# The order of projection products on TensorE during a linear recurrence

## The chip, the cores and the metric

The kernel runs on one core of one Trainium2 chip. The metric is the device time of one execution in microseconds (us). Engines: TensorE (PE; its weight loads are PEld), VectorE (DVE), ScalarE (ACT), GpSimd (POOL, which here mostly issues transfers) and SyncE (SP, which issues transfers).

## The reference

Two residual layers over 528 tokens (16 prepended and 512 of the input) of width 2048, in float32. The first layer is a convolution module beside a sparse attention; the change does not touch it. The second is a gated linear recurrence (HGRN2) of 16 heads of width 128. The part of it that matters here:

```python
def odd_mixer(hn, w_in, lb, norm_g, w_out):
    q, fz, i, g = split_last(hn @ w_in, (D_REC, D_REC, D_REC, D_REC))
    log_f = jnp.logaddexp(jnp.log(lb), jnp.log1p(-lb) + jax.nn.log_sigmoid(fz))
    k = (1.0 - lb) * jax.nn.sigmoid(-fz)
    o = hgrn2_chunkwise(heads(jax.nn.silu(q)), heads(log_f), heads(k), heads(i))
    o = o * lax.rsqrt(jnp.mean(jnp.square(o), -1, keepdims=True) + RMS_EPS)
    ...
    return o @ w_out

# hgrn2_chunkwise, one step over a chunk of tokens:
    b = jnp.cumsum(g_c, axis=2)
    o_inter = jnp.einsum('bhtk,bhkv->bhtv', q_c * jnp.exp(b), state)
    attn = jnp.einsum('bhtk,bhtsk,bhsk->bhts', q_c, jnp.exp(diff), k_c)
    o_intra = jnp.einsum('bhts,bhsv->bhtv', attn, v_c)
    state = (jnp.exp(b_last)[..., None] * state
             + jnp.einsum('bhsk,bhsv->bhkv', k_c * jnp.exp(b_last[:, :, None] - b), v_c))
```

`fz` (the forget gate) and `i` (called `v` in the kernel) are the two projections that are made head by head while the recurrence runs. `q` and `g` are made before it.

## The kernel before

Each float32 operand of a large product is split into a high and a low half in float16, and a product is three matmuls for each of its contraction steps: high by high (L214), high by low (L215) and low by high (L216). Weights come by transfers into a raw float32 tile. ACT rounds it to the high half `wh` and DVE takes the difference as `wl` (L174 and L175 for plain stripes, L1369 and L1370 for pairs). There are three buffers of `wh` and `wl`, and three PSUM banks `mps` that take the products' results in turn.

The recurrence is the loop over heads, `fz` and `v` of each head first and then the head itself (`rec_head`).

- The odd heads use `projections`: two plain stripes, for `fz` (j = 0) and for `v` (j = 2). A stripe is two column parts of 264 tokens by two halves of the contraction, four products of 24 matmuls. DVE takes `fz` out of its banks, ACT takes `v` out (L1013).
- The even heads from 2 on use `paired`: both projections by one Strassen step, seven products of 24 matmuls, 272 columns each, in the order 1, 5, 2, 4, 6, 7, 3. Their weights are sums and differences of the quarters of both stripes. POOL's accumulating transfers make the sums (L1382, L1386, L1389), and the weight tiles hold the products' weights in the pairs 1 and 5, 2 and 4, 7 and 6, and 3 alone. ACT takes products 1, 5 and 4 out of PSUM (L1401, L1403 for the two that go to `v`), DVE the others, with `u` as the running sum.
- `rec_head` does the recurrence of a head: float16 key-query matmuls of 64 columns (L1195 to L1197, results `s`, of which ACT and DVE make the attention tile `A`), float32 transposes of `v` (L1231, with the copy to `vt` by ACT, L1229), state matmuls (`st`, L1332, which need `kk` of ACT L1328) and outputs (`po`, L1343 and L1344, squared by ACT into `so`, L1350). ACT and DVE also make the gates (`ta`, `tb`), the decayed keys and queries (`kt0h`, `kt1h` and their low halves) between these.

Every engine runs its instructions strictly in its own order. That order is not the source's: a scheduler makes it from the dependences, its own picture of the times, and priorities, which the code gives in bands (`WGT` for weights, `EVAC` for taking results out of PSUM, `SIDE` for the head's own work). The seven products of `paired` are called inside the `EVAC` band, the products of plain stripes outside. So before the change the scheduler starts products of a pair while the odd head's `v` stripe in front of it still has matmuls left.

Of the kernel before, what the change touches and what calls it, by code (L numbers as in the profile page):

```python
# [74 lines left out]
def trunk_kernel(ctx: ExitStack, tc: tile.TileContext, x: bass.AP, w: bass.AP, wukv: bass.AP,  # L75
# [3 lines left out]
    V, S, G, P, Q = nc.vector, nc.scalar, nc.gpsimd, nc.tensor, nc.sync  # L79

    def band(level):
        return tc.high_priority(level * 1000000)
# [66 lines left out]
        V.tensor_scalar(vec[:, V_RG:V_RG + 16], vec[:, V_RG:V_RG + 16], 0.5, None, op0=OP.mult)  # L149


    loaded, halved = [], []

    def weight_tiles():
        return [wpool.tile([128, 2064], F16, name=n, bufs=3)[:, :2048] for n in ("wh", "wl")]
# [24 lines left out]
    def weights_of(at, items):  # L180

        if at % 2 == 0 or not ahead:
            ahead.clear()
            for i, half in enumerate(load_two([product_weights(*it) for it in items[at:at + 2]])):
                ahead[at + i] = half
        return ahead[at]
# [16 lines left out]
    def stripe_half(weights, X, parts, n, half, m=128):  # L203

        hi, lo = weights
        for o, sl in parts:
            products(o[:m], hi, lo, [[x[:, sl] for x in X[half * 8 + k]] for k in range(8)], n == 0, n == 1, m)

    def products(o, hi, lo, X, start, stop, m=128):

        issued = []
        for k, (xh, xl) in enumerate(X):
            ws = slice(k * 128, k * 128 + m)
            P.matmul(o, hi[:, ws], xh, start=start and k == 0, stop=False)  # L214
            P.matmul(o, hi[:, ws], xl, start=False, stop=False)  # L215
            issued.append(P.matmul(o, lo[:, ws], xh, start=False, stop=stop and k == len(X) - 1))  # L216
        return issued

    def evac(dst, parts, rstd):
# [208 lines left out]
    for k in range(KT):  # L428
        xh, xl = X0[k]
        st, sp = k == 0, k == KT - 1  # L430
        for parts, s, m in ((kwp, S_KW, KWM), (c0p, S_C, 128)):
            hi, lo = first[s][k // 8]
            ws = slice(k % 8 * m, k % 8 * m + m)
# [480 lines left out]
    for at, (pr, m) in enumerate(turns):  # L914
        u, c0, c1 = us[pr], C[pr], C[8 + pr]
        o = (mps if at % 7 < 3 else ps1)()[:, :HT]
        with band(WGT):
            hi, lo = weights_of(at, [(EPAIRS[p], m2) for p, m2 in turns])
        products(o, hi, lo, forms0[FORM[m]], True, True)
        with band(EVAC):  # L920
            if m == 2:
# [37 lines left out]
    def on_tile(k, wide=False):  # L959
        t = hp.tile([128, T if k < 6 or k in (12, 14) else SEQ], F32, name=f"on{k}", bufs=1)  # L960
        return t if wide else t[:, :SEQ]
# [83 lines left out]
    def strassen(turns, pairs, results, finished):  # L1045
# [5 lines left out]
        for n, (m, pr) in enumerate(turns):  # L1051
            o = (mps if made[0] % 7 < 3 else ps1)()[:, :HS]
            with band(WGT):
                hi, lo = weights_of(n, items)
            made[0] += 1
            products(o, hi, lo, [[x[:, NM:] for x in pair] for pair in gforms[FORM[m]]], True, True)
            if made[0] % 3 == 2:
                paced_steps(lsteps, 1, o, gpp)
# [58 lines left out]
    def head_inputs(h):  # L1117
        fz, v = [ht([128, T], F32, name, 2) for name in ("fz", "v")]
        if h in QT and h not in QDRAM:
            return fz, QT[h], v  # L1120
        q = ht([128, SEQ], F32, "q", 2)
        if h in QT:
            G.dma_start(q, qd[QDRAM.index(h)])
        return fz, q, v
# [289 lines left out]
    for h in range(16):  # L1414
        if h < 2:
            inputs[1] = inputs[1] or head_inputs(1)
        else:
            inputs[h] = head_inputs(h)
        fz, q, v = inputs[h]
        if h:  # L1420
            (paired if h in PAIRED else projections)(h, fz, v)
        if h in (8, 9):
            ON.append(on_tile(h))
            G.dma_start(ON[h], gd[h - 8])
        with band(SIDE):
            rec_head(h, fz, q, v)
# [166 lines left out]
    for at, (pr, m) in enumerate(turns):  # L1593
        n0, n1 = 2 * pr, 2 * pr + 1
        o = (mps if at % 7 < 3 else ps1)()[:, :HS]
        with band(WGT):
            hi, lo = weights_of(at, [(OPAIRS[p], m2) for p, m2 in turns])
# [6 lines left out]
        issued = products(o, hi, lo, forms[FORM[m]], True, True)  # L1604
# [126 lines left out]
```

## Time and profile before

| | |
|---|---|
| median of 3 runs | 1782.55 us (1781.63 to 1782.58) |
| profiled execution | 1785.19 us |
| its span | 1783.4 us |
| mean TensorE clock granted | 0.982 |
| recurrence with its projections, about | 1080 to 1600 us of the span |

The rows quoted below are of the profiled execution. A row of a timeline gives the start in us, the duration in us, engine, line, operation, the tile written and the tiles read, the shape, and in brackets the idle time just before it and what ended that. A row of waits gives the total in us, how often, and the longest. A row of windows gives the length of the stretch, the busy time of PE, PEld, DVE, ACT and POOL with their instructions, the granted clock (1.00 is full), the share of the transfer engines, and GB/s. Line numbers are those of the kernel before. In the changed kernel the same lines stand one further down (L215 to L217 for the three matmuls) or three (L1016 for L1013, L1372 for L1369, L1404 for L1401).

### The profile page before, as it was taken

How to read it: one execution, taken by the hardware profiler on the slowest of the kernel's cores; microseconds unless marked ns; L12 is line 12 of the kernel's file. 1: busy time of each engine (PE TensorE's matmuls, PEld its weight loads, DVE VectorE, ACT ScalarE, POOL GpSimd, SP SyncE). 2: the span in 40 equal slices, each digit the busy share in tenths (PEclk: the TensorE clock that was granted, in tenths of full speed). 3: DMA queues.
4: the chain of work that ended last, by engine and by line, in shares of the span. 5: the costliest groups of instructions: out<-in, count | busy, mean ns of one | idle time of the engine just before them, and what ended most of it. 6: DMA issues, size and time to landing. Idle time of an engine off the chain costs nothing. (4 is left out here: it accounts for less than half of the span.)

```text
span 1783.4 us, 37905 instructions
## 1 busy us (share of the span) xinstructions
PE 1730.9 (97%) x15616; PEld 1451.5 (81%) x15616; DVE 1442.3 (81%) x2412; ACT 967.1 (54%) x1782; POOL 293.8 (16%) x501
## 2 busy tenths in 40 slices
PE   9999999999999999999999999899999999989997
PEld 8775688888888888888888888787887787657886
DVE  7699899999478579699776587788888888879876
ACT  7333532235446455457534456666776777756553
POOL 1020233123342211102110101111111111100000
PEclk9999999999999999999999999999999999989998
DMA  9578688979999857877899978677677766524764
GB/s 361 171 235 268 176 237 201 251 227 232 233 247 303 209 185 273 252 253 264 277 281 297 290 237 236 181 188 195 153 193 181 188 159 181 158 80 151 261 217 141
DMA packets 108126, 393.34 MB, mean 221 GB/s; under 512 B 14768, under 2 KB 22616, under 8 KB 106096
## 3 DMA queue, kind: packets, MB, share of 16 engines
q0 software_dynamic: 36944, 157.91, 37.9%
q1 hardware_dynamic: 70720, 232.81, 36.9%
q8 instruction: 122, 2.00, 0.4%
q14 instruction: 52, 0.43, 0.1%
q10 hardware_dynamic: 288, 0.19, 0.0%
HBM read 369.07 MB, written 136.53 MB: 284 GB/s over the span
## 5 line engine op out<-in xcount | busy, mean ns | idle before, releaser
L215 PE MATMUL mps<-xl,wh 128*128 128x264 f16 (+3 forms) x2560 | 730.2, 285 | 1.6 <-DVE xl L242 1.6
L216 PE MATMUL mps<-xh,wl 128*128 128x264 f16 (+3 forms) x2560 | 730.2, 285 | 0.0
L214 PE MATMUL mps<-xh,wh 128*128 128x264 f16 (+3 forms) x2560 | 728.8, 286 | 0.0
L174 ACT ACTIVATE wh<-w 128x2048 f16<-128x2048 f32 (+1 forms) x174 | 331.0, 1902 | 306.7 <-PE mps L215 202.7
L175 DVE SCALAR_TENSOR_TENSOR wl<-w,wh 128x2048 f16<-128x2048 f32 (+1 forms) x174 | 396.9, 2281 | 113.8 <-ACT wh L174 113.4
L215 PEld LDWEIGHTS <-wh 128*128 128x128 f16 x4128 | 406.4, 98 | 100.6 <-issue 20.3
L216 PEld LDWEIGHTS <-wl 128*128 128x128 f16 x4128 | 406.5, 98 | 85.6 <-issue 3.1
L214 PEld LDWEIGHTS <-wh 128*128 128x128 f16 x4128 | 406.7, 99 | 81.7 <-issue 1.0
L632 DVE SCALAR_TENSOR_TENSOR z<-u,vec,z 128x528 f32<-128x528 f32 x240 | 179.3, 759 | 2.1
L214 PE MATMUL mps<-gh,wh 128*128 128x272 f16 (+1 forms) x368 | 108.1, 294 | 18.4 <-ACT v L1013 17.0
L289 POOL DMA_DIRECT2D ws<-in_w_dram x116 | 106.5, 1123 | 113.0 <-DMA ws<-ws 65.0
L215 PE MATMUL mps<-gl,wh 128*128 128x272 f16 (+1 forms) x368 | 108.0, 293 | 0.0
L216 PE MATMUL mps<-gh,wl 128*128 128x272 f16 (+1 forms) x368 | 107.8, 293 | 0.0
L1369 ACT ACTIVATE wh<-w 128x2048 f16<-128x2048 f32 (+1 forms) x28 | 47.6, 1699 | 62.9 <-DMA w<-in_w_dram 32.1
L216 PE MATMUL s<-xh,wl 128*128 128x256 f16 (+1 forms) x288 | 78.8, 274 | 0.0
L214 PE MATMUL s<-xh,wh 128*128 128x256 f16 (+1 forms) x288 | 78.8, 274 | 0.0
L215 PE MATMUL s<-xl,wh 128*128 128x256 f16 (+1 forms) x288 | 78.8, 274 | 0.0
L1370 DVE SCALAR_TENSOR_TENSOR wl<-w,wh 128x2048 f16<-128x2048 f32 (+1 forms) x28 | 56.5, 2018 | 20.8 <-ACT wh L1369 20.5
L331 POOL MEMSET pace<- 128x1 f32 x52 | 5.9, 113 | 352.9 <-ACT pace L330 352.9
L695 POOL DMA_DIRECT2D L<-mask x32 | 30.3, 947 | 165.0 <-DMA L<-bdram 104.3
L1318 DVE TENSOR_TENSOR kq<-kq,e 128x512 f32<-128x512 f32 (+1 forms) x80 | 55.5, 693 | 1.1
L222 DVE SCALAR_TENSOR_TENSOR gt<-mps,rstd 128x264 f32<-128x264 f32 (+1 forms) x70 | 31.2, 447 | 24.9 <-PE mps L216 24.6
(659 smaller groups left out, 3345.0 us busy)
## 6 DMA issues: line engine op xcount, KB each, us to landing
ws<-in_w_dram POOLq DMA_DIRECT2D x158, 512.0 KB, 8.4
w<-in_w_dram SPq DMA_DIRECT2D x72, 1024.0 KB, 7.5
w<-in_w_dram SPq DMA_DIRECT2D x118, 512.0 KB, 5.3
w<-ws SPq DMA_DIRECT2D x116, 512.0 KB, 4.9
ws<-ws POOLq DMA_DIRECT2D x58, 512.0 KB, 5.3
w<-in_w_dram POOLq DMA_DIRECT2D x28, 512.0 KB, 6.1
ws<-in_w_dram SPq DMA_DIRECT2D x16, 512.0 KB, 8.1
sq<-mbd POOLq DMA_DIRECT2D x16, 264.0 KB, 4.1
```

The costliest lines, as they stand in the source:

```text
L174: halved[:] = [S.activation(hi[:, :n], w32[:, :n], AF.Copy, scale=WS), V.scalar_tensor_tensor(lo[:, :n], w32[:, :n], WS, hi[:, :n], op0=OP ...
L175: V.scalar_tensor_tensor(lo[:, :n], w32[:, :n], WS, hi[:, :n], op0=OP.mult, op1=OP.subtract)]
L214: P.matmul(o, hi[:, ws], xh, start=start and k == 0, stop=False)
L215: P.matmul(o, hi[:, ws], xl, start=False, stop=False)
L216: issued.append(P.matmul(o, lo[:, ws], xh, start=False, stop=stop and k == len(X) - 1))
L222: V.scalar_tensor_tensor(dst[:, sl.start - o:sl.stop - o], p[:dst.shape[0]], IW, rstd[:dst.shape[0], sl], op0=OP.mult, op1=OP.mult)
L289: return G.dma_start(wsum[pair, m], src, accum_op=OP.add, max_dma_last_dim=4096)
L632: V.scalar_tensor_tensor(z, u[:, j:j + T], col(V_CW + i * CW + j), z, op0=OP.mult, op1=OP.add)
L695: return G.dma_start(biased[h, t][:, :wk(t)], M[t], accum_op=OP.add)
L1318: V.tensor_tensor(both, both, by, op=OP.mult)
L1369: halved[:] = [S.activation(hi[:, :n], raw[:, :n], AF.Copy, scale=WS), V.scalar_tensor_tensor(lo[:, :n], raw[:, :n], WS, hi[:, :n], op0=OP ...
L1370: V.scalar_tensor_tensor(lo[:, :n], raw[:, :n], WS, hi[:, :n], op0=OP.mult, op1=OP.subtract)]
```

## The change

A list `stream` is filled between heads 1 and 15. While it is, the first matmul of each product is told to stand on TensorE behind the last matmul of the product before it in the source. It concerns the scheduler's order alone.

```diff
-    loaded, halved = [], []
+    loaded, halved, stream = [], [], []
...
         for k, (xh, xl) in enumerate(X):
             ws = slice(k * 128, k * 128 + m)
-            P.matmul(o, hi[:, ws], xh, start=start and k == 0, stop=False)
+            with tc.issue_after(stream[-1].ins) if stream[1:] and k == 0 else ExitStack():
+                P.matmul(o, hi[:, ws], xh, start=start and k == 0, stop=False)
             P.matmul(o, hi[:, ws], xl, start=False, stop=False)
             issued.append(P.matmul(o, lo[:, ws], xh, start=False, stop=stop and k == len(X) - 1))
+        if stream:
+            stream.append(issued[-1])
         return issued
...
         if h:
+            if h == 1:
+                stream.append(None)
             (paired if h in PAIRED else projections)(h, fz, v)
+            if h == 15:
+                stream.clear()
```

TensorE has the same matmuls in both kernels, and SP's order is the same. TensorE's order differs from head 1 on; ACT's and DVE's differ with it, POOL's in a few rows.

In the rows that follow the numbers behind names tell tiles apart: `mps_19454` is the bank of the last part of head 13's `v` stripe; of head 14's pair, `mps_19824` is product 1, `mps_19850` product 5, `mps_19902` product 4, `mps_19928` product 6 and `mps_19982` product 3.

TensorE where head 14's pair begins. Before:

```order
L216 MATMUL mps_19454<-xh_9531,wl_19457 128x264
L214 LDWEIGHTS wh_19456
L214 MATMUL mps_19454<-xh_9566,wh_19456 128x264
L215 LDWEIGHTS wh_19456
L215 MATMUL mps_19454<-xl_9567,wh_19456 128x264
L214 LDWEIGHTS wh_19802
L214 MATMUL mps_19824<-xh_9456,wh_19802 128x272
```

and now:

```order
L216 MATMUL mps_19454<-xl_10265,wh_19456 128x264
L217 LDWEIGHTS wl_19457
L217 MATMUL mps_19454<-xh_10264,wl_19457 128x264
L215 LDWEIGHTS wh_19802
L215 MATMUL mps_19824<-xh_9456,wh_19802 128x272
L216 LDWEIGHTS wh_19802
L216 MATMUL mps_19824<-xl_9457,wh_19802 128x272
```

Product 1 started in the middle of the `v` stripe's last part (contraction tile `xh_9566` of the first half), and now starts behind its last matmul (`xh_10264`).

ACT around the copies out of PSUM of heads 13 and 14. Before:

```order
L1369 ACTIVATE wh_19819<-w32_19797 128x1024
L1350 ACTIVATE so_18424,ss_18425<-po_18402 128x128 x4
L1229 ACTIVATE vt0_13706<-sv_19126,rt1n_13703 128x128
L1251 ACTIVATE kt1h_13717<-kq1_13709 128x2x8x32
L1191 ACTIVATE kt0h_13713<-kq0_13705 128x256
L1251 ACTIVATE kt0h_13713<-kq0_13705 128x512
L1351 ACTIVATE ss_18425<-ss_18425,eps_r_78 128x4
L174 ACTIVATE wh_20250<-w32_20249 128x2048
L1013 ACTIVATE v_19344<-mps_19454 128x264
L1401 ACTIVATE v_19794<-mps_19850 128x264
L1403 ACTIVATE v_19794<-mps_19902 128x264
```

and now:

```order
L174 ACTIVATE wh_20356<-w32_20355 128x2048
L1353 ACTIVATE so_18424,ss_18425<-po_18402 128x128 x4
L1232 ACTIVATE vt0_13706<-sv_19126,rt1n_13703 128x128
L1313 ACTIVATE A_18697<-s1_18814 32x4x32
L1254 ACTIVATE kt0h_13713<-kq0_13705 128x512
L1194 ACTIVATE kt0h_13713<-kq0_13705 128x256
L1313 ACTIVATE A_18697<-s1_18814 32x4x32
L1313 ACTIVATE A_18697<-s1_18814 64x4x64
L1215 ACTIVATE ta_19559<-ta_19559 128x528
L1354 ACTIVATE ss_18425<-ss_18425,eps_r_78 128x4
L1404 ACTIVATE v_19794<-mps_19850 128x264
L1406 ACTIVATE v_19794<-mps_19902 128x264
```

The copy of the `v` stripe's last part (L1013) stood directly ahead of those of products 5 and 4 and has moved far ahead of these rows; the split of the second stripe of head 15 (`wh_20356`) stood behind the copies and now stands in front of them, where it takes the weight buffer that product 7 leaves.

TensorE just ahead of product 3 of head 14, now:

```order
L1198 MATMUL s1_18814<-kt1l_13718,kt1h_13717 128x64
L1199 LDWEIGHTS kt1h_13717
L1199 MATMUL s1_18814<-kt1h_13717 128x64
L1200 LDWEIGHTS kt1l_13718
L1200 MATMUL s1_18814<-kt1h_13717,kt1l_13718 128x64
L1234 MATMUL sv_19135<-ident_73,v_18894 128x128
L215 LDWEIGHTS wh_19819
L215 MATMUL mps_19982<-xh_10005,wh_19819 128x272
```

The transpose of head 13's `v` (`sv_19135`) stood in front of product 6 before, behind the `v` stripe's last matmul, and now stands in front of product 3.

ACT behind head 8's pair. Before:

```order
L174 ACTIVATE wh_17655<-w32_17654 128x2048
L1369 ACTIVATE wh_18002<-w32_17997 128x2048
L1251 ACTIVATE kt1h_13717<-kq0_13705 128x2x128x2
L1310 ACTIVATE A_16000<-s1_16117 32x4x32 x2
L1310 ACTIVATE A_16000<-s1_16117 64x4x64
L1203 ACTIVATE ta_17309<-fz_17091 128x528
L1204 ACTIVATE ta_17309<-ta_17309 128x528
L1205 ACTIVATE ta_17309<-ta_17309 128x528
L1328 ACTIVATE kk_16153<-st_16148 128x512
```

and now:

```order
L174 ACTIVATE wh_17655<-w32_17654 128x2048
L1194 ACTIVATE kt0h_13713<-kq0_13705 128x512
L1372 ACTIVATE wh_18002<-w32_17997 128x2048
L1254 ACTIVATE kt1h_13717<-kq0_13705 128x2x128x2
L1313 ACTIVATE A_16000<-s1_16117 32x4x32 x2
L1313 ACTIVATE A_16000<-s1_16117 64x4x64
L1331 ACTIVATE kk_16153<-st_16148 128x512
```

The split of head 10's first weights (`wh_18002`) stands ahead of `kk` in both. On TensorE the state matmuls that need `kk` stood behind 48 matmuls of head 9's `fz` stripe, and now stand behind 30.

## The prediction

> **What bounds the kernel now.** I read the totals first, then TensorE's waits in the recurrence (1080 to 1580 us), then the engines' rows around the longest wait.
>
> ```profile
> PE 1730.9 (97%) x15616; PEld 1451.5 (81%) x15616; DVE 1442.3 (81%) x2412; ACT 967.1 (54%) x1782; POOL 293.8 (16%) x501
> ```
>
> TensorE is the bound, and the change gives it no matmul more or less. So only its idle time and its clock can move. The waits are few:
>
> ```profile
> PE mps L214 <- ACT v L1013: 17.0, 5, 3.4
> PE sv L1231 <- ACT vt L1229: 4.9, 1, 4.9
> ...
> PE mps L214 <- ACT v L1403: 1.4, 1, 1.4
> ```
>
> The columns are total us, times and the longest. The five 3.4s stand in heads 6, 8, 10, 12 and 14, the 4.9 in head 2, the 1.4 in head 4. Each 3.4 also costs clock:
>
> ```profile
> 1176.68 0.28 PE L214 MATMUL mps<-gh,wh 128*128 128x272 f16 x1 [1.42 <-ACT v L1403]
> ...
> 1232.51 0.39 PE L214 MATMUL mps<-gh,wh 128*128 128x272 f16 x1 [3.40 <-ACT v L1013]
> 1232.69 0.43 PE L215 MATMUL mps<-gl,wh 128*128 128x272 f16 x1
> ...
> 1238.35 0.28 PE L216 MATMUL mps<-gh,wl 128*128 128x272 f16 x1
> ...
> 1238.70 0.28 PE L216 MATMUL mps<-gh,wl 128*128 128x272 f16 x1
> ```
>
> ```profile
> 1232.50:1238.30 5.80, 5.79 (x26) 3.90 (x26) 5.80 (x10) 4.18 (x12) 0.84 (x1) 0.50 1.05 299
> ...
> 1294.00:1355.50 61.50, 58.14 (x626) 50.39 (x626) 51.49 (x90) 42.99 (x99) 10.52 (x16) 0.94 0.68 175
> ```
>
> In the windows' rows the clock is the third number from the end: 0.50 for the 5.84 us from 1232.51 to 1238.35, so 2.9 us of work lost, and 0.94 over a whole pair of heads (61.50 us). After the idle of 1.42 matmuls run at full rate at once. Rows at full clock stand 0.116 us apart (1238.35 to 1238.70, three steps).
>
> Why 3.4: product 6 of a pair needs the third PSUM bank, which the last part of the odd head's v stripe leaves by ACT's copy L1013. ACT's queue holds it up:
>
> ```profile
> 1349.46 0.38 PE L1343 MATMUL po<-st,kq 128*128 128x128 f32 x2
> 1349.68 0.39 PE L1344 MATMUL po<-vt,A 128*128 128x128 f32 x2
> ...
> 1351.94 0.33 PE L1231 MATMUL sv<-ident,v 128*128 128x128 f32 x1
> ```
>
> ```profile
> 1349.54 1.06 ACT L1369 ACTIVATE wh<-w 128x1024 f16<-128x1024 f32 x1 [2.68 <-PE mps L215]
> 1350.50 0.26 ACT L1350 ACTIVATE so<-po 128x128 f32<-128x128 f32 x1
> ...
> 1351.50 0.38 ACT L1229 ACTIVATE vt<-sv,rt1n 128x128 f32<-128x128 f32 x1
> 1351.75 0.65 ACT L1251 ACTIVATE kt1h<-kq 128x512 f16<-128x512 f32 x1
> 1352.27 0.51 ACT L1191 ACTIVATE kt0h<-kq 128x256 f16<-128x256 f32 x1
> 1352.62 0.78 ACT L1251 ACTIVATE kt0h<-kq 128x512 f16<-128x512 f32 x1
> 1353.24 0.30 ACT L1351 ACTIVATE ss<-ss,eps_r 128x4 f32<-128x4 f32 x1
> 1353.41 1.92 ACT L174 ACTIVATE wh<-w 128x2048 f16<-128x2048 f32 x1
> 1355.21 0.40 ACT L1013 ACTIVATE v<-mps 128x264 f32<-128x264 f32 x1
> ...
> 1356.37 0.63 ACT L1212 ACTIVATE ta<-ta 128x528 f32<-128x528 f32 x1
> 1356.90 0.61 ACT L1251 ACTIVATE kt1h<-kq 128x512 f16<-128x512 f32 x1
> ```
>
> The weight split of W3 starts ACT at 1349.54, when product 4 gives up a weight buffer. The copy comes out 5.67 us later (1349.54 to 1355.21), and TensorE's last work before it starts at 1351.94 and takes 0.33: idle 3.40. The steps between these starts are my durations: so x4 1.00, vt 0.25, kt1h 0.52, kt0h 0.35 and 0.62, ss 0.17, wh 1.80, v 0.27, ta 0.53.
>
> **The change, part by part.** It adds no wait, no instruction and no transfer. It only tells the scheduler that from head 1 to 15 a product's first matmul stands behind the previous product's last one. What moves:
>
> 1. The v stripe no longer has paired products in its middle. Its banks empty before the pair, so the five waits on L1013 and the 1.42 on L1403 cannot come in this form: between a bank's products stand two others, 48 matmuls by 0.116 = 5.6 us. The copy it waits for then decides, and ACT's order has moved too.
>
> 2. Heads 10, 12 and 14. Behind product 7, ACT's next row is now the next stripe's split (wh L174, for which product 7 must have freed the weights), then so x4, then vt, and TensorE's next transpose (L1234 in the new lines) needs that vt: 1.80 + 1.00 + 0.25 = 3.05, with 0.15 for the hand-over (the 0.2 us between 1355.48, the end of v's 0.27, and the matmul at 1355.67 bounds it) 3.2. TensorE has only two po steps (0.22 each, 1349.46 to 1349.68) and eight key-query matmuls left, under 0.8 together. Idle 2.4. Then product 3 waits for product 5's bank, whose copy (L1404 now) stands behind A x3, kt0h twice, ta and ss: 0.83 + 0.62 + 0.35 + 0.53 + 0.17, and its own 0.27 and 0.2: 2.97, less the transpose's 0.27: idle 2.7. Together 5.1 where 3.40 was: +1.7 each, **+5.1**. The 0.83 for A is from this fence:
>
> ```profile
> 1369.14 1.91 ACT L1369 ACTIVATE wh<-w 128x2048 f16<-128x2048 f32 x1 [3.23 <-DMA w<-in_w_dram]
> 1370.96 0.67 ACT L1251 ACTIVATE kt1h<-kq 128x512 f16<-128x512 f32 x1
> 1371.53 0.92 ACT L1310 ACTIVATE A<-s 32x128 f32<-32x128 f32 x3
> 1372.36 0.63 ACT L1203 ACTIVATE ta<-fz 128x528 f32<-128x528 f32 x1
> ...
> 1374.24 0.58 ACT L1328 ACTIVATE kk<-st 128x512 f32<-128x512 f32 x1
> 1374.72 0.72 ACT L1210 ACTIVATE kq<-tb,logk 128x528 f32<-128x528 f32 x1
> ```
>
> 3. Head 6 has the same order, but some 0.8 us more of work in front of each of the two waits (more po pairs and key-query matmuls): idle 2.0 + 2.3 = 4.3, **+0.9**.
>
> 4. Heads 4 and 8. There the copies stand early in ACT's queue and nothing of point 2 arises. But behind the pair ACT reaches the split of the next pair's first weights (wh L1372) before kk, and TensorE now has only 30 product matmuls ahead of the state matmuls that need kk, where it had 48. The split waits for loads:
>
> ```profile
> 1109.17 0.87 POOL L1389 DMA_DIRECT2D w<-in_w_dram  x1 [2.51 <-DVE wl L1370]
> ...
> 1164.09 1.42 POOL L1389 DMA_DIRECT2D w<-in_w_dram  x1
> ```
>
> ```profile
> 1114.53 1.06 ACT L1369 ACTIVATE wh<-w 128x1024 f16<-128x1024 f32 x1 [3.64 <-DMA w<-in_w_dram]
> 1130.24 1.91 ACT L1369 ACTIVATE wh<-w 128x2048 f16<-128x2048 f32 x1 [7.85 <-DMA w<-in_w_dram]
> 1175.30 1.06 ACT L1369 ACTIVATE wh<-w 128x1024 f16<-128x1024 f32 x1 [8.58 <-DMA w<-in_w_dram]
> ```
>
> ```profile
> 1116.87 0.33 SPq L1380 DMA_DIRECT2D w<-in_w_dram  x1
> ...
> 1352.90 0.34 SPq L1380 DMA_DIRECT2D w<-in_w_dram  x1
> ```
>
> ```profile
> 1371.08 2.29 DVE L1370 SCALAR_TENSOR_TENSOR wl<-w,wh 128x2048 f16<-128x2048 f32 x1 [0.63 <-ACT wh L1369]
> w<-in_w_dram POOLq DMA_DIRECT2D x28, 512.0 KB, 6.1
> ```
>
> From T0, the end of the v stripe: the split of W7 and W6 takes 1.80 + 2.29; POOL's addition for W3 5.4 (1109.17 to 1114.53) to 11.2 (1164.09 to 1175.30), I take the page's median 6.1; W3's split 2.3: T0 + 12.5. The loads and the addition that follow take 13.4 (1116.87 to 1130.24) to 16.3 (1352.90 to 1369.14): T0 + 26 to 29. kk ends 1.80 + 0.57 + 0.83 + 0.48 = 3.7 later, T0 + 29.6 to 32.5. TensorE gets there after seven products (168 x 0.116 = 19.5), 1.7 of small matmuls and 5.3 of the 30 product matmuls and the small ones among them: T0 + 26.5. Idle 3.1 to 6.0; I take 4.4, near the middle, since the rows give no reason for either end. Head 8: 4.4 for 3.40, **+1.0**. Head 4: 4.4 for 1.42, and 2.9 of clock that was not lost before, **+5.9**.
>
> 5. Head 2's 4.92 comes from the wait of 7.85 on loads above, ahead of the first pair; the loads' order on SP is unchanged: 0, from -1 to +1.5. The end of the recurrence: 0, ±3. Elsewhere the new order leaves TensorE margins of 0 to 1 us behind its evacuations on DVE and ACT: 0, up to +1 for each of seven pairs.
>
> Clock: every pair of heads that had a 3.4 still has one stretch of idle time of that size or more, so its 2.9 stays. If both parts of point 2's idle time drop the clock apart, up to 2.9 more; if neither does, 2.9 less (the second rival).
>
> The sum is 5.1 + 0.9 + 1.0 + 5.9 = **+12.9**. The profiled execution took 1785.19 us (span 1783.4), so the changed kernel's would be 1798; the runs' median is 2.6 below it, 1782.55, and gives **1795**. A measurement of this kernel tells about 0.2% (3.6 us) from no change: faster is below 1779, slower above 1786.
>
> **The rivals.**
>
> *The stalls vanish (the other side).* If ACT reaches v's copies within the 5.6 us that two products take, the five waits go, 17.0, with their five losses of clock, 14.5: -31.5, 1751. For it: each bank's product ended 5.6 us earlier. Against it: the copy L1404 stands behind a split that itself waits for product 7, the very product in front of the one that needs the bank; it can come no sooner than 1.80 after it. It decides at product 3 of heads 10 to 14: if ACT's split is past before product 7 ends. Chance 0.08.
>
> *The idle time is there but in parts too short to drop the clock.* The idle of 1.42 dropped nothing, 3.40 did. If 2.0 to 2.7 do not, heads 10, 12 and 14 give 5.1 - 3.4 - 2.9 = -1.2 each, head 6 gives 0.9 - 2.9 = -2.0; with +1.0 and +5.9 that is +1.3: 1784, no change. For it: no row between 1.42 and 3.40 shows which way it goes. Against it: between the two parts TensorE does a single transpose of 0.27, so 5.4 us hold 0.3 of work. Chance 0.10. The Trainium skill, page "TensorE: Matmul & The Clock Gate", Part 1 (the HAM clock gate), has the clock fall after at least one wholly idle window of about 3.4 us, and the window runs freely. By that rule two gaps under 2.8 us would leave the clock up, and the sum would be this rival's. Here a gap of 3.40 dropped the clock five times in five, which a free-running window wholly without work could do only by luck, so the trace speaks for a rule that drops sooner.
>
> *W3's sum lands late everywhere.* Product 7's bank needs DVE's sum u, which now stands behind W3's low half; with 11.2 for POOL's addition in place of 6.1 it is up to 4.9 late, at four places 20: 1815. One of the two rows has it so. Against it: the row of 11.2 lay beside POOL's stripe loads, and the median of 28 is 6.1. Chance 0.13.
>
> **How the numbers follow.** The forecast's own case has 0.69, with 1785 to 1806 as its own range (heads 4 and 8 from 3.1 to 6.0, the margins of point 5). Below 1779 lie the first rival and a third of the second: 0.11. Within 0.2% lie the rest of the second and the lowest part of the forecast: 0.11. Slower: 0.78. The range from 1780 to 1812 leaves out the first rival, the low edge of the second and half of the third, 0.18 together.
>
> **What would show it.** Right: waits of TensorE at the transpose for vt (about 2.4) and at a product for v L1404 (about 2.7), in heads 10, 12 and 14 one behind the other; ACT's wh L174 released by TensorE just behind product 7; wh L1372 waiting for loads after heads 4 and 8, with TensorE waiting for kk; none for v L1016 any more; as much time at clock 0.50 as before, or more. Wrong: no wait at product 3 (the split came early), full clock behind the two parts, or product 7 waiting for u.

## The result, and the profile after

The changed kernel takes 1798.43 us (median of 4 runs, 1797.19 to 1800.05) beside 1782.57 for the kernel before on the same chip: a ratio of 1.0084, 95% interval 1.0065 to 1.0104, so 0.65 to 1.0% slower. Its profiled execution took 1798.05 us with a span of 1796.3, 12.9 more than the one of before.

The totals of the changed kernel's page:

```profile
PE 1733.2 (96%) x15616; PEld 1454.0 (81%) x15616; DVE 1442.6 (80%) x2412; ACT 970.7 (54%) x1782; POOL 292.6 (16%) x501
```

TensorE does the same 15616 matmuls, busy 2.3 us longer in the whole span; the rest of the 12.9 is idle time. Its windows over most of the recurrence show the same, before (from 1080 to 1565) and after (1080 to 1578):

```profile
1080.00:1565.00 485.00, 461.59 (x4854) 390.26 (x4853) 398.51 (x682) 338.01 (x739) 76.42 (x120) 0.96 0.70 183
```

```profile
1080.00:1578.00 498.00, 459.90 (x4817) 388.83 (x4815) 395.39 (x679) 339.86 (x736) 75.75 (x120) 0.96 0.68 176
```

Idle is the length less the first busy time: 23.4 before, 38.1 after. The second window holds 37 matmuls fewer, since in this profile the changed kernel entered the recurrence 4.4 us sooner (the first transposes of `on` start at 1077.35, before at 1081.81). The waits of TensorE in the changed kernel (1080 to 1580), which answer to those of before:

```profile
PE sv L1234 <- ACT vt L1232: 15.1, 5, 6.3
PE mps L215 <- ACT v L1404: 12.8, 6, 3.2
PE st L1335 <- ACT kk L1331: 9.0, 3, 4.7
```

The wait for the v stripe's copy (L1013, now L1016) is gone. The waits for three other things that ACT makes have grown in its place. On TensorE's timeline, from head 2 to head 14:

```profile
1129.98 0.48 PE L1234 MATMUL sv<-ident,v 128*128 128x128 f32 x1 [6.26 <-ACT vt L1232]
1188.88 0.38 PE L1335 MATMUL st<-vt,kk 128*128 128x128 f32 x1 [3.57 <-ACT kk L1331]
...
1300.64 0.28 PE L215 MATMUL mps<-gh,wh 128*128 128x272 f16 x1 [3.16 <-ACT v L1404]
1316.55 0.58 PE L1335 MATMUL st<-vt,kk 128*128 128x128 f32 x1 [4.70 <-ACT kk L1331]
...
1491.70 0.33 PE L1234 MATMUL sv<-ident,v 128*128 128x128 f32 x1 [2.49 <-ACT vt L1232]
1494.49 0.38 PE L215 MATMUL mps<-xh,wh 128*128 128x272 f16 x1 [2.46 <-ACT v L1404]
```

The last two are head 14's, and ACT's rows there are the queue that the prediction walked through:

```profile
1488.45 1.91 ACT L174 ACTIVATE wh<-w 128x2048 f16<-128x2048 f32 x1 [3.76 <-PE mps L216]
1490.27 0.26 ACT L1353 ACTIVATE so<-po 128x128 f32<-128x128 f32 x1
...
1491.26 0.38 ACT L1232 ACTIVATE vt<-sv,rt1n 128x128 f32<-128x128 f32 x1
1491.51 0.25 ACT L1313 ACTIVATE A<-s 32x128 f32<-32x128 f32 x1
...
1493.88 0.28 ACT L1354 ACTIVATE ss<-ss,eps_r 128x4 f32<-128x4 f32 x1
1494.07 0.37 ACT L1404 ACTIVATE v<-mps 128x264 f32<-128x264 f32 x1
```

ACT waited 3.76 us for product 7 to give up its weight buffer, then split the next v stripe's weights, while so, vt and the copy of product 5 stood behind. TensorE's transpose waits for vt and product 3 for that copy.

### The profile page after: what moved, and what is told of

Read it like the earlier page. It is cut to its first block, busy times and chain, and to the rows that moved or that the text cites. A ratio compares the mean times of both kernels' runs of the same rounds, so it can differ in the third digit from the quotient of the medians.

```text
span 1796.3 us, 37920 instructions
## 1 busy us (share of the span) xinstructions
PE 1733.2 (96%) x15616; PEld 1454.0 (81%) x15616; DVE 1442.6 (80%) x2412; ACT 970.7 (54%) x1782; POOL 292.6 (16%) x501
## 5 line engine op out<-in xcount | busy, mean ns | idle before, releaser
L215 PE MATMUL mps<-xh,wh 128*128 128x264 f16 (+3 forms) x2560 | 737.0, 288 | 8.5 <-ACT v L1404 8.5
L174 ACT ACTIVATE wh<-w 128x2048 f16<-128x2048 f32 (+1 forms) x174 | 330.8, 1901 | 291.3 <-PE mps L216 190.8
L215 PE MATMUL mps<-gh,wh 128*128 128x272 f16 (+1 forms) x368 | 101.9, 277 | 4.5 <-ACT v L1404 4.3
L216 PE MATMUL mps<-gl,wh 128*128 128x272 f16 (+1 forms) x368 | 101.9, 277 | 0.0
L217 PE MATMUL mps<-gh,wl 128*128 128x272 f16 (+1 forms) x368 | 101.9, 277 | 0.0
L1372 ACT ACTIVATE wh<-w 128x2048 f16<-128x2048 f32 (+1 forms) x28 | 47.5, 1695 | 65.6 <-DMA w<-in_w_dram 60.7
L1254 ACT ACTIVATE kt1h<-kq 128x512 f16<-128x512 f32 x64 | 40.5, 633 | 25.5 <-DVE kq L1321 24.3
```

The costliest lines, as they stand in the source:

```text
L174: halved[:] = [S.activation(hi[:, :n], w32[:, :n], AF.Copy, scale=WS), V.scalar_tensor_tensor(lo[:, :n], w32[:, :n], WS, hi[:, :n], op0=OP ...
L1254: S.activation(hi, src, AF.Copy)
L1372: halved[:] = [S.activation(hi[:, :n], raw[:, :n], AF.Copy, scale=WS), V.scalar_tensor_tensor(lo[:, :n], raw[:, :n], WS, hi[:, :n], op0=OP ...
```

## The experiments

Each ran on one chip beside the kernel before; ratios are to it. "The changed kernel" is the base unless the text says otherwise. In the runs with edits the same lines stand up to seven further down than in the kernel before (L1237 or L1236 for L1234, L1407 for L1404). Theory A says that ACT's order makes the idle time: what TensorE waits for is ready to be done, and stands behind a weight split that itself waits for something. Theory B says that products back to back with three banks wait in any case.

**One edge per pair.** Only product 1 of each pair is held behind the v stripe.

```diff
...
-            if h == 1:
-                stream.append(None)
+            if h in PAIRED:
+                stream[:] = [None, last_v[0]]   # the edge of product 1 alone
...
```

> The kernel before with one part of the change: only product 1 of each pair is held behind the last matmul of the v stripe in front of it; all other products are free. If the boundary is what acts: 1796 to 1801, with the same waits as the changed kernel. If the order inside stripes and pairs acts as well: between 1783 and 1794.

Measured: 1796.16 us, ratio 1.0078 (1.0066 to 1.009), with the same waits (13.4 for v, 12.9 for vt, 6.8 for kk). The boundary between stripe and pair carries the change; what the other edges add is within the two intervals.

**The next v stripe's split behind the copies.**

```diff
-            ps = stripe(S_FQV + 3 * h + j, X1)
+            with tc.issue_after(copies[-1].ins) if copies and j == 2 else ExitStack():
+                ps = stripe(S_FQV + 3 * h + j, X1)
...
-            S.activation(v[:, left], product(4)[:, :HT], AF.Copy)
+            copies[:] = [S.activation(v[:, left], product(4)[:, :HT], AF.Copy)]
```

> The changed kernel, with the split of the next v stripe (wh L174) queued on ACT behind the copies of products 5 and 4. Theory A (ACT's queue): the changed kernel's idle in heads 6, 10, 12 and 14 (3.75, 3.77, 4.81 and 4.95 us, 17.3 together) comes from this split standing ahead of vt and of the copies. Without it vt comes 1.8 earlier and its wait falls to 0.6 or less; A, kt0h and ss still stand ahead of the copies, so product 3 keeps about 2: idle falls by 7 to 9, and where the clock no longer drops by up to 9 more: 1782 to 1791. Theory B (spacing): products stand back to back with three banks, so TensorE finds no free bank whatever ACT does first: no change, 1798 within 3.

Measured: 1785.13 us, 1.0025 (1.0012 to 1.0037). TensorE's order keeps every edge of the change, and most of the loss is back: 13 us by the medians, 10.5 by the ratios (1.0084 less 1.0025, of 1782). Head 14 in this kernel:

```profile
1483.46 0.33 PE L1237 MATMUL sv<-ident,v 128*128 128x128 f32 x1 [0.61 <-ACT vt L1235]
1485.65 0.28 PE L215 MATMUL mps<-xh,wh 128*128 128x272 f16 x1 [1.86 <-ACT v L1407]
```

The waits are 0.61 where 0.6 was expected and 1.86 where 2 was. In the four heads aimed at, 17.3 us of idle time became 10.0. The rest of the gain lies elsewhere: the wait of 4.70 for kk in head 8 is gone too (that of head 4 stays, at 3.85), while 2.7 for u came in three pairs. Theory B falls.

**kk ahead of the next pair's first split,** in all pairs, and only behind heads 4 and 8.

```diff
...
-            W[1], W[5] = split_raw(raw)
+            with tc.issue_after(decay[h - 5].ins) if h > 5 else ExitStack():   # or: if h in (6, 10)
+                W[1], W[5] = split_raw(raw)
```

> The changed kernel, with the split of a pair's first weights (wh L1372, which waits for loads) queued on ACT behind kk of the head whose state matmuls are due there. Theory A: the waits of TensorE for kk (3.57 in head 4, 4.70 in head 8) go, with about 2 us of clock: 1786 to 1791. Rival C: the split then comes late itself, and the same time is lost at product 1 of the next pair, or the recurrence only moves the wait: 1796 to 1802.

> The changed kernel with that edge behind heads 4 and 8 alone. The two waits for kk (3.57 and 4.70 us) and their clock go: 8 to 11 less than 1798, 1787 to 1791. If the gain of the run with kk first in all pairs came from heads 10 to 14: 1794 to 1798.

Measured: 1790.49 (1.0042, 1.0028 to 1.0055) and 1790.72 (1.0038, 1.0024 to 1.0052). With two edges the waits for kk behind heads 4 and 8 are gone (0.7 in the stretch, where 9.0 was), and heads 12 and 14 keep 2.49 + 2.46 and 2.49 + 2.32. So the split that waits for loads, in front of kk, is worth about the 8 us expected. With the edge in all pairs heads 12 and 14 wait only 1.4 to 1.5 and 1.1 each, which the medians don't show.

**A third buffer for v.** Product 5's copy writes the buffer that holds the v of two heads earlier until that is transposed.

```diff
-        fz, v = [ht([128, T], F32, name, 2) for name in ("fz", "v")]
+        fz, v = ht([128, T], F32, "fz", 2), ht([128, T], F32, "v", 3)
```

> The changed kernel with a third buffer for v. Theory D (the buffer): the copy of product 5 can't be made before the v of two heads earlier has been transposed, and that transpose waits for vt, which stands behind the split; with a third buffer the copy is free when product 5 ends. Then product 3's waits go (1.84, 1.86, 2.32 and 2.46, and 3.16 in head 8: 11.6 of idle, and with them clock): 1776 to 1788. Theory A without D: the copies stay behind the split, 1794 to 1800.

Measured: 1808.17, 1.0146 (1.0129 to 1.0163): a miss, outside both ranges. Product 3's waits in heads 10 to 14 are gone, and product 6 waits 0.99 in each for product 5's copy. The last pair's last product ended 14 us sooner than in the changed kernel (1485.5 for 1499.7), though TensorE waited 7.68 for u in head 8. But from there to the end it took 317 us, where the changed kernel took 297 (1802.5 less 1485.5, 1796.3 less 1499.7). ACT's rows show why: six heads' kk come behind that product, where the changed kernel has five. With one more buffer the recurrence ran a head further behind its projections, and that head's work stands uncovered at the end.

**Both edits together.**

> The changed kernel with both edits of the first two experiments: the next v stripe's split behind the copies of products 5 and 4, and a pair's first split behind kk. If the two stalls are of different places and add: 1798 - 13 - 8 = 1777, between 1772 and 1782. If the second edit's gain came from the same heads as the first's (its trace showed less idle in heads 10 to 14 too): 1781 to 1788.

> As the run with both edits, but kk stands ahead of the next pair's first split only behind heads 4 and 8, where the changed kernel waited for kk; the next v stripe's split stays behind the copies. Theory E: the run with both edits lost its gain because the first split of every pair came late, and with it the loads of that buffer and W3's sum, so that TensorE waited for u. With two such places only, the pairs of heads 12 and 14 keep their loads in time: 1774 to 1785. If the two edits can't stand together for another reason (ACT's order around the copies): 1795 or more.

Measured: 1816.33 (1.018, 1.0157 to 1.0204) and 1816.37 (1.0176, 1.0157 to 1.0195). The first lies far outside both of its ranges. The second lies in its own second range (1795 or more, another reason), and with it theory E fell: with the first split early in heads 12 and 14 it is as slow. TensorE's waits in the first of the two:

```profile
PE mps L215 <- DVE u L1411: 19.0, 3, 9.1
PE sv L1237 <- ACT vt L1235: 13.6, 6, 4.2
PE mps L215 <- DVE fz L1409: 7.0, 1, 7.0
```

And POOL's queue there, ahead of head 12's W3 (L1396), with ACT's split of it:

```profile
1410.89 0.51 POOL L290 DMA_DIRECT2D ws<-ws  x1 [4.40 <-DMA ws<-in_w_dram]
1414.95 0.81 POOL L292 DMA_DIRECT2D ws<-in_w_dram  x1 [3.55 <-DMA ws<-ws]
1415.51 1.18 POOL L1396 DMA_DIRECT2D w<-in_w_dram  x1
```

```profile
1423.93 1.06 ACT L1375 ACTIVATE wh<-w 128x1024 f16<-128x1024 f32 x1 [12.95 <-DMA w<-in_w_dram]
```

W3's sum did not wait for its own operands (no bracket): the split that must be done before it (L1376 on VectorE, from 1407.69, 2.29 long) had ended at 1410.0, and the sum came 5.5 later and took 8.4 more until ACT could split it. It stood behind a chain of copies and sums of the output projection's weights (`ws`), each step of which waits for the one before, and which a row of the recurrence starts. That is theory F.

**Those sums behind the recurrence.** They are moved, and the output projection waits for them, so only the recurrence is read.

```diff
-        paced_steps(osteps, 4, vt[:, 1, :], hrp)
+        paced_steps(osteps, 64 if h == 15 else 0, vt[:, 1, :], hrp)
```

> The run with both edits (1816), with POOL's sums of the output projection's weights (64 steps of copies and accumulating transfers, four per head) all moved behind the recurrence. The output projection then waits for them, so the total says nothing; the recurrence is what is read. Theory F (POOL's queue): W3's sum is late because it stands behind those four-step chains; without them it is issued when the split of W7 and W6 is done and lands in about 5.5 us, and the waits for u (4.00, 9.12, 5.93) and for fz (6.97) fall under 2: a pair takes 59 to 61 us from one product 3 to the next, where that run took 67. Theory E (the first split comes late): the waits for u stay, 65 or more.

> The changed kernel with the same move; again only the recurrence is read. Theory F: behind heads 4 and 8 two of these sums were issued 1.4 and 2.6 us ahead of W3's, which then took 10 us to land; without them W3's lands in about 5.5, the wait of 3.16 in head 8 (ACT v L1404) goes and the one of 1.16 in head 4 too, while the two waits of heads 10, 12 and 14 (2.3 to 2.5 each) stay, since they come from ACT. Otherwise 3.16 stays.

The totals were 1841 and 1843 us, one run each. With both edits, W3's sum of head 10 is issued on its own operands and is split 5.5 us later:

```profile
1327.59 0.85 POOL L1396 DMA_DIRECT2D w<-in_w_dram  x1 [6.79 <-DVE wl L1376]
```

```profile
1333.13 1.06 ACT L1375 ACTIVATE wh<-w 128x1024 f16<-128x1024 f32 x1 [2.23 <-DMA w<-in_w_dram]
```

The waits for u and fz from VectorE fall to 2.1 and 0.6 in all, the longest 1.43. From one product 3 to the next, heads 6 to 14, it takes 59.7, 60.7, 61.6 and 62.5 us, where the run with both edits took 65.0, 66.7, 73.1 and 68.7 (59 to 61 was expected). On the changed kernel the 3.16 of head 8 and the 1.16 of head 4 vanish, and heads 12 and 14 keep 2.49 + 2.32 and 2.50 + 2.46, as theory F has it:

```profile
PE mps L215 <- ACT v L1404: 8.5, 4, 2.5
PE st L1335 <- ACT kk L1331: 5.0, 2, 3.1
```

The wait for kk behind head 8 falls from 4.70 to 3.12, that behind head 4 from 3.57 to 1.87. In all seven pairs of this run W3's sum takes 5.3 to 5.6 us from issue to split. Theory F is shown as far as these sums are the cause. The runs don't separate POOL's order from the slower landing of a sum issued right behind others: the move takes both away.

**The other way round: the kernel before, with its own stall treated.** First the next fz stripe's split (L174) behind the copies, then W3's split behind the v stripe's copy as well, then that copy on VectorE in place of both.

```diff
+            with tc.issue_after(copies[-1].ins) if copies and j == 0 else ExitStack():
                 ps = stripe(S_FQV + 3 * h + j, X1)
...
```

> The kernel before (no edges on TensorE) with the split of the next fz stripe (wh L174) queued on ACT behind the copies of the pair's products 5 and 4, and so behind the v stripe's copy L1013. Theory A: the 3.40 waits fall by the split's 1.80 to 1.6 each, -9, and the clock then drops for a shorter time or not at all, -5 to -14: 1759 to 1768. If the v stripe's own bank or the spacing of products sets the wait: 1779 to 1784.

Measured: 1780.42, 0.9983 (0.997 to 0.9996); the profiled span is 1774.8.

```profile
PE mps L214 <- ACT v L1016: 8.0, 5, 1.6
```

```profile
1287.50:1293.00 5.50, 5.50 (x48) 4.65 (x48) 5.50 (x9) 5.50 (x13) 0.00 (x0) 1.00 0.97 204
...
1355.00:1414.70 59.70, 56.15 (x629) 49.30 (x627) 50.90 (x90) 42.48 (x97) 10.52 (x17) 1.00 0.73 187
```

The wait is 1.60, as expected, and behind it the clock stays at 1.00 (third number from the end). Yet the time is far from the 1759 to 1768 expected, and in the range of the other branch, whose cause the 1.60 rules out. A pair took 61.50 us with TensorE busy 58.14 before, and takes 59.70 with 56.15 now: the clock's 2.0 is won, and the 1.8 of idle comes back in new waits (1.01 for the decay e, up to 1.37 for kk). And the last product 3 ended 15.8 us sooner (1473.7 for 1489.5; 3.6 of that was there when the recurrence began, at 1078.2 for 1081.8), the end came only 8.6 sooner in these profiles and 2.7 by the medians: 301 us follow that product, where 294 did. Why the end takes longer I did not follow. It is the fastest version measured here, by 0.04 to 0.3%.

> As the last one, and the split of W3 (wh L1369, 1.06) is queued behind the v stripe's copy L1013 as well. Theory A: 0.6 of the 3.40 is left and no clock is lost: 1751 to 1760, some 6 below the run with one split moved. If W3's split is then late for product 3: no better than that run.

> The kernel before, with the copies of the odd heads' v stripes (L1013) made by VectorE and not by ScalarE, so that they leave ACT's queue. If ACT's queue alone made the five waits of 3.40: they fall to 1 or less and no clock is lost: 1752 to 1766. If VectorE, which is busy 51 of 61.5 us in a pair, then comes late with low halves and gates: 1772 to 1790.

Measured: 1788.38 (1.0025, 1.0014 to 1.0037) and 1789.32 (1.0032, 1.0017 to 1.0048). The first range of each expectation was missed. The times lie in the ranges of the other branches, whose causes the traces bear out only in part. With the copy and W3's split exchanged the wait is 1.4 still: in head 8 ACT waits 3.24 us for TensorE's po instead, and the rows from so to ss stand ahead of the copy as before. W3's split holds up product 3 in head 4 alone, by 1.2 us. TensorE waits for kk behind five pairs:

```profile
PE st L1335 <- ACT kk L1331: 11.6, 5, 3.2
PE sv L1234 <- ACT vt L1232: 10.2, 2, 6.0
PE mps L214 <- ACT v L1016: 7.1, 5, 1.5
```

With the copies on VectorE four of the five waits are gone and one of 1.34 is left, and the time is lost at product 5's copy (2.28), kk (3.22), kt1l (2.98) and smaller ones. Of these kt1l is a low half of VectorE, as the expectation's other branch has it; the first two are ACT's. What each moved row made late beyond these, I did not follow.

## Why the prediction was right, point by point

**The sum.** +12.9 was forecast; the profiles differ by 12.9 and the medians by 15.9. That the first agrees so closely is luck. Of the forecast 10.0 was idle time and 2.9 clock. TensorE's waits up to the last product 3 grew by 12.8 (23.35 to 36.13), and the work lost to the clock did not grow (about 16 us before, 15 after, estimated from the granted clock behind each wait). From its first transposes to that product's end the recurrence took 14.6 us longer (422.3 for 407.7), what follows took 2.7 longer, and the changed kernel's profile had entered the recurrence 4.4 sooner. No term of the forecast has this last: all other profiles of this document enter it at 1077.4 to 1080.0, so the late one is that of the kernel before.

**Points 1 and 2 (heads 10, 12, 14), the 3.40s go and two others come.** Right in mechanism, shown by the run with the split moved. The sizes: 2.49 + 2.32 and 2.49 + 2.46 in heads 12 and 14 against 2.4 + 2.7. Head 10 has 1.91 + 1.86. The prediction took its queue to be theirs, but it is head 6's: ACT's split there does not wait for product 7, and no ta row stands ahead of the copy.

**Point 3 (head 6).** 1.91 + 1.84 = 3.75, forecast 4.3. The working does not give its own number: 0.8 us more of work in front of each wait would leave 1.6 + 1.9, and 2.0 + 2.3 takes off 0.4 each.

**Point 4 (heads 4 and 8).** The waits for kk came at 3.57 and 4.70, forecast 4.4 each. The step that failed is the sentence that the copies there "stand early in ACT's queue and nothing of point 2 arises": product 7 waits for product 5's copy, 1.16 in head 4 and 3.16 in head 8. The copy stood behind W3's split, which waited for W3's sum:

```profile
1284.77 0.85 POOL L292 DMA_DIRECT2D ws<-in_w_dram  x1 [3.74 <-DMA ws<-in_w_dram]
1285.97 0.83 POOL L292 DMA_DIRECT2D ws<-in_w_dram  x1 [0.36 <-DMA ws<-in_w_dram]
1287.39 0.89 POOL L1392 DMA_DIRECT2D w<-in_w_dram  x1 [0.58 <-DVE wl L1373]
```

```profile
1297.46 1.06 ACT L1372 ACTIVATE wh<-w 128x1024 f16<-128x1024 f32 x1 [8.38 <-DMA w<-in_w_dram]
1298.42 1.89 ACT L174 ACTIVATE wh<-w 128x2048 f16<-128x2048 f32 x1
1300.22 0.37 ACT L1404 ACTIVATE v<-mps 128x264 f32<-128x264 f32 x1
```

The sum took 10.1 us from issue to split behind two others, where I took the page's median of 6.1. Without those others it took 5.5 (head 8 in the run with these sums moved). So the term lacked 4.3 us of idle time over both heads; the shorter waits of heads 6 and 10 made up for 1.9 of it, and those for kk for 0.5.

**Point 5 (head 2).** 6.26 for 4.92: +1.3, inside its bounds.

**The clock.** The forecast was that the 2.9 of every pair stays. At half rate (the matmuls' spacing in the timeline) the changed kernel lost 2.6, 2.5, 1.8 and 2.6 us in heads 6, 10, 12 and 14. In head 8 no clock was lost behind the 3.16, but 1.5 behind the wait for kk (granted clock 0.53 over 3.1 us), and in head 4 it was 1.7 (0.60 over 4.2), where 2.9 was forecast.

**The rivals.** That the stalls vanish did not happen: the split did wait for product 7 in heads 12 and 14, as its "against" had it. That two short parts would not drop the clock is refuted in heads 6, 10, 12 and 14; here two of them, with head 8 between:

```profile
1241.80:1247.00 5.20, 5.20 (x24) 3.38 (x24) 4.83 (x11) 3.97 (x11) 2.31 (x3) 0.50 0.84 254
1300.60:1306.00 5.40, 5.36 (x47) 4.52 (x47) 5.40 (x10) 3.44 (x6) 0.84 (x1) 1.00 0.96 335
1369.00:1374.00 5.00, 4.92 (x22) 3.19 (x22) 5.00 (x13) 4.10 (x12) 2.32 (x3) 0.50 0.88 240
```

The first and third rows follow 1.91 + 1.84 and 1.91 + 1.86 with a transpose between, the second follows the single 3.16. The rule quoted from the Trainium skill ("TensorE: Matmul & The Clock Gate", Part 1) asks for an idle window of about 3.4 us. With the transpose counted as idle the two gaps make 4.1 us, so these rows speak against it only if a transpose counts as work. The run with the split moved does not agree with it either way: 0.61 and 1.86 with a transpose of 0.33 between make 2.8 us, and the clock fell in most heads. That W3's sum lands late did happen, at two places in place of four, and it reached TensorE by ACT's copy and not by u. In the runs with both edits TensorE waited for u, as that rival described it.

## What to carry to other kernels

Before an edge is added on the engine that bounds a kernel, look in the other engines' queues at what the scheduler will then put ahead of the row that this engine waits for. A weight split that waits for a buffer or a load is worst there, since everything behind it on its engine waits too. And two such repairs don't add: each moves rows on all engines, and a shared queue (here POOL's sums) or the tail of a recurrence that lags can take back more than both gave.

## What the runs showed of the hardware

The clock is not lost by one long gap alone. A gap of 0.61 and one of 1.86, with only a transpose of 0.33 between, halved it in three heads of the run with the split moved (in a fourth it was 0.74 and 1.86), and not in the last of them. The windows behind the gaps of heads 12 and 14:

```profile
1424.90:1429.00 4.10, 4.10 (x23) 2.94 (x23) 4.10 (x9) 3.95 (x7) 2.30 (x3) 0.63 0.53 160
1485.60:1488.30 2.70, 2.65 (x23) 2.24 (x23) 2.70 (x8) 2.70 (x4) 1.11 (x2) 1.00 0.84 156
```

A single gap of 1.60 never did (five of five at 1.00), one of 3.16 did not, one of 3.40 did each time in the kernel before. The fall can come after work has resumed: in the first of these two rows TensorE ran at 0.99 for 1.1 us and then at 0.52 for 3.5. Where it fell behind such gaps, the work lost was about 1.5 to 1.8 or 2.5 to 2.9 us. Why the same pair of gaps drops it in one head and not in another, the runs don't show.

An accumulating transfer of 512 KB into the weight buffer took 5.3 to 5.6 us from issue to its reader's start in all seven pairs of the changed kernel with the other sums moved. Right behind one such sum it took 8.4 (head 12 with both edits), behind two 9.1 and 10.1 (heads 4 and 8 of the changed kernel).
